# A two-layer hybrid decoder trunk on one core: DMAs of split-ahead weights issued by GpSimd instead of SyncE, and shorter steps in the first stage

## The chip, the cores and the metric

The kernel runs on one core of a Trainium2 chip. The metric is the device time of one execution in microseconds (us). Before the change the median of two runs is 2187.45 us (2185.61 to 2189.3). One more execution was profiled and took 2193.86 us; the profile's rows are of that one.

## The reference

Two decoder layers over 1024 tokens of width 1024, all in float32. Layer 0 mixes tokens by gated linear attention (GLA, 4 heads), layer 1 by sparse attention (an indexer chooses 256 keys per query, 16 heads). After each mixer comes a layer norm of the residual sum and a gated addition of a per-layer embedding `p`.

```python
# layer 0
h = x @ w_in                      # q, k: 1024 wide each; v, z: 2048 each; a: 16
g = log_sigmoid(a @ w_a2 + b_a) / 16
# per head, in chunks, state S (256 x 512):
o_c = q_c S + tril(q_c k_c^T) v_c ;  S = S * decay + k_c^T v_c
o = o * rsqrt(mean(o*o) + eps) * gn_g
y = (o * silu(z)) @ w_out
# layer 1
q, k, v, z, qi, ki, wi = split(x @ w_in)
score = sum_h relu(qi_h . ki) * wi_h ;  idx = top_k(score, 256)
y = (softmax(q . k[idx]) v[idx] * silu(z)) @ w_out
# after each
x = layer_norm(ALPHA * x + y)
x = x + (p[i] @ ple_w[i]) * sigmoid(x @ ple_gate_w[i])
```

## The kernel before, in words

**Precision.** TensorE multiplies in float32r. To keep float32's accuracy each operand is split into a high part (ScalarE copies it to float32r) and a low part (VectorE subtracts the high part), and each product is three matmuls: high by high, high by low, low by high. So every weight has to be loaded, split into two tiles and kept until it is used.

**Stages.** (1) The *front* (`front_phase`) multiplies x by the weights of q, k and most of z of layer 0 for all 1024 tokens. It does so in pairs of blocks (`class Pair`) by a Strassen-like scheme: seven products of 12 matmuls instead of eight, from sums and differences of operands. (2) *Layer 0* runs in two halves of 512 tokens (half 0, half 1), each over four heads. Head h has core steps (`core_steps`: scores `s1`, state `s2`, output `s3`, turning `s4`, for four chunks c of 128 tokens); between them run the v projection of head h+1 (`v_phase`) and the output projection of head h-1 (`out_phase`). Each half ends with the layer norm (`norm_steps`) and a tail; the tail of half 0 also holds small projections of layer 1. (3) *Layer 1* runs in two halves over 16 heads and two tails.

**Order of work.** Every engine executes its instructions in the order in which the program emits them, and SyncE (SP) issues all DMAs in such an order too: an instruction that waits holds up everything behind it on its engine or queue. The program emits TensorE's matmuls in sequence and keeps a clock of its own, `fl.now`, in units of estimated us: each matmul of 512 columns adds 512/2400 (line 60). All other work is placed by that clock: `after(dt, f)` emits f when the clock has moved on by dt; `req` puts a step off until its condition holds; pacers are called after each few matmuls.

- The *operand queue* of the front: for each pair 18 steps (allocation, sums, high parts, low parts, load), one emitted every `pacing["gap"]` units (line 1567: 1.3 from the third pair on). The queue is refilled with the steps of the next pair after product 1 of the running one (the third pair: after product 6). When a product needs an operand whose step has not yet been emitted, `todo` emits steps until it has.
- *Split-ahead* (`Weights.split_ahead`, lines 228 to 257) splits the 65 weight tiles of layer 1 and of its small projections, in order, in the background: 30 in the front (line 1581), one step every 1.4 units, and 35 in layer 0 (line 1670), every 2.06 units. For each half of a tile (a *cut*, 256 KB) it loads `pst` (three buffers), lets ScalarE write `phi` (line 248), stores `phi` to DRAM (line 250), loads the cut after the next (line 238), lets VectorE subtract (line 252) and stores the low part (line 254). Three steps per cut; `bg3.finish()` at the end of the front (line 1588) and of layer 0 (line 1761) emits whatever is left at once. Layer 1 then loads finished parts (line 176).
- *Kept parts* (line 205): the v and output weights of layer 0, split in half 0, are stored to DRAM for half 1: 32 tiles, two stores each.
- *Turning by DRAM* (`squares_out`, `squares_in`, `gate`; lines 724 to 752): for most chunks the output `ot` is stored to DRAM as `od` in four DMAs (line 727), read back turned as `uf` (line 733, two buffers) 4.0 units later, and gated by VectorE (line 752) another 4.0 units later. The other chunks are turned on TensorE in `s4` through the PSUM bank `oT`, which `v_phase` also uses.
- GpSimd computes `rs`, the scale of a head's output rows (lines 756 and 758, in `made`, when a turned block is ready; used at line 803), and `rstd` in the layer norms (lines 841 to 844), and clears some tiles (`wa2f` at line 1617, for instance).

At the start of layer 0 and for each head `g_load` (line 473) loads `wa2f`, from which the decays are made.

Of the kernel before, what the change touches and what calls it, by code (L numbers as in the profile page):

```python
# [144 lines left out]
class Weights:  # L145
# [16 lines left out]
    def step(self):  # L162
        n, i = self.ns, self.part
        if n == self.stop:
            return False
        whole = n not in self.staged and self.seq[n][0] in self.ahead
        if n >= self.nu + (3 if whole and self.seq[self.nu - 1][0][0] not in ("do", "o") else 2):
            return False
        if i == 0:
            if not whole:  # L170
                self.loads(n + 1)
            if n not in self.parts:
                self.reserve(n)
        if whole:
            for part, there in zip(self.parts[n], self.ahead[self.seq[n][0]]):
                self.nc.sync.dma_start(part.bitcast(F32), there)
            self.ns += 1
            self.loads(min(self.ns + 1, self.nu + 3))
            return True
        st = self.staged[n]  # L180
        hi, lo = self.parts[n]
        if n == 0:
            i = (0, 2, 1, 3)[i]
        c = slice((i % 2) * 512, (i % 2) * 512 + 512)
        key = self.seq[n][0]
        gain = None
        if key[0] == "o":
            row = 4 * key[1] + 2 * key[3] + i % 2
            gain = self.gains[:, row:row + 1]
        if i < 2:  # L190
            self.nc.scalar.activation(hi[:, c], st[:, c], AF.Copy, scale=1.0 if gain is None else gain)
        elif gain is None:
            self.nc.vector.tensor_sub(lo[:, c], st[:, c], hi[:, c].bitcast(F32))
        else:
            self.nc.vector.scalar_tensor_tensor(lo[:, c], st[:, c], gain, hi[:, c].bitcast(F32),
                                                op0=OP.mult, op1=OP.subtract)
        self.part = (self.part + 1) % 4
        if self.part == 0:
            if key in self.keep:
                there = [self.dram.tile([128, 1024], F32, name=x) for x in ("whs", "wls")]  # L200
                self.keep.remove(key)

                def store():
                    for x, part in zip(there, (hi, lo)):
                        self.nc.sync.dma_start(x, part.bitcast(F32))
                    self.ahead[key] = there
                self.after(1.6, store)
            self.staged.pop(n)
            self.ns += 1
            self.after(1.5, lambda: self.loads(self.ns + 2))  # L210
        return True
# [16 lines left out]
    def split_ahead(self, keys, pool, hi_pool):  # L228

        w = dict(self.seq)  # L230
        cuts = [(key, slice(c, c + 512)) for key in keys for c in (0, 512)]
        tiles = {}

        def load(i):
            if i < len(cuts):
                key, c = cuts[i]
                tiles[i] = pool.tile([128, 512], F32R, tag="pst", name="pst", bufs=3)
                self.nc.sync.dma_start(tiles[i].bitcast(F32), w[key][:, c])
        load(0)
        load(1)  # L240
        yield
        yield
        for i, (key, c) in enumerate(cuts):
            st = tiles.pop(i)
            if not c.start:
                there = [self.dram.tile([128, 1024], F32, name=n) for n in ("whs", "wls")]
            hi = hi_pool.tile([128, 512], F32R, tag="xst", name="phi", bufs=2)
            self.nc.scalar.activation(hi, st.bitcast(F32), AF.Copy)  # L248
            yield
            self.nc.sync.dma_start(there[0][:, c], hi.bitcast(F32))  # L250
            load(i + 2)
            self.nc.vector.tensor_sub(st, st.bitcast(F32), hi.bitcast(F32))  # L252
            yield
            self.nc.sync.dma_start(there[1][:, c], st.bitcast(F32))
            if c.start:
                self.ahead[key] = there
            yield

    def take(self, key):
# [33 lines left out]
def trunk_kernel(ctx, tc, x_tok, x_T, p_T, pos, freq, g_q, g_k, g_v, g_z, g_a, g_a2, g_ba, g_gn, g_o,  # L293
# [281 lines left out]
    def qk_phase(u):  # L575
# [23 lines left out]
            after(0.7, lambda: split(qh[:, 1], ql[:, 1], q[:, 1], done))  # L599
        chain((0, query(0)), (0.6, query(1)), (0.6, key(0)), (0.6, key(1)))  # L600

    def core_steps(u):
        h, half = u["h"], u["half"]
        v = u["v"]
# [84 lines left out]
        def s3(c):  # L689
            def f():  # L690
                cs = slice(c * 128, c * 128 + 128)
                fl.req(("A", c) in st, v[c] is not None, not has_state(c) or ("S", c) in st and "qhl" in u)
                fl.ripe(st["At", c] + 1.6)
                Ah, Al = st.pop(("A", c))
                vh, vl = v[c]
                ps = pp.tile([128, 512], F32, tag="o", name="o")
                ops = [(Ah, vh), (Al, vh), (Ah, vl)]
                if has_state(c):
                    qh, ql = u["qhl"]
                    for d, (sh, sl) in enumerate(st.pop(("S", c))):  # L700
                        ops += [(qh[:, d, cs], sh), (ql[:, d, cs], sh), (qh[:, d, cs], sl)]
                for i, (l, r) in enumerate(ops):
                    mm(ps, l, r, i == 0, i == len(ops) - 1)
                ot = lp.tile([128, 512], F32, tag="ot", name="ot", bufs=2)
                if by_square(c):
                    dve.transpose(ot.rearrange("p (m b i) -> p b m i", m=4, b=4), ps)  # L706
                    after(2.2, lambda: squares_out(c, ot))
                else:
                    dve.tensor_copy(ot, ps)
                junk = lp.tile([128, 512], BF16, tag="junk", name="junk")  # L710
                act.activation(junk, ps, AF.Square, accum_out=u["ss"][:, c:c + 1])  # L711
                st["o", c] = ot
                st["ot", c] = fl.now
                u["spent"].add(c)
                if c == 3:
                    u["late"] = True
                if c < 3:
                    after(0.3, lambda: make_S(c + 1))
            return f
# [4 lines left out]
        def squares_out(c, ot):  # L724
            od = dp.tile([4, 32, 4, 128], F32, tag="od", name="od", bufs=4)
            for a in range(4):
                nc.sync.dma_start(od[:, :, a].rearrange("m r x -> r m x"),
                                  ot[32 * a:32 * a + 32].rearrange("p (m x) -> p m x", m=4))

            def squares_in():  # L730
                fl.req(h == 0 or u["prev"].get("out", 0) > c)
                uf = lp.tile([128, 512], F32, tag="uf", name="uf", bufs=2)
                nc.sync.dma_start(uf, od.rearrange("m r a x -> (m r) (a x)"))
                after(4.0, lambda: gate(c, uf))
            after(4.0, squares_in)

        def gate(c, uf):
            fl.req("z" in u)
# [12 lines left out]
            z = u["z"][:, :, c * 128:c * 128 + 128].rearrange("p b (a i) -> p b a i", a=4)  # L751
            chain((0, lambda: dve.tensor_mul(turned, turned, z)), (0.8, high), (0.9, low))

        def made(c, uh, ul):
            rc = slice(c, c + 1)
            pool.tensor_scalar(u["rs"][:, rc], u["ss"][:, rc], ALPHA ** 2 / 512.0, ALPHA ** 2 * EPS,
                               op0=OP.mult, op1=OP.add)
            pool.tensor_tensor(u["rs"][:, rc], u["rs"][:, rc], mhalf[:, rc], op=OP.pow)
            u["u"][c] = uh, ul

        def s4(c):
            def f():
# [1 line left out]
                    return  # L764
                cs = slice(c * 128, c * 128 + 128)
                fl.req(h == GH - 1 or units[h + 1].get("turns"))
                fl.req(("o", c) in st, "z" in u, h == 0 or u["prev"].get("out", 0) > c)
                fl.ripe(st["ot", c] + 1.1)
                ot = st.pop(("o", c))
                ps = pp.tile([128, 4, 128], F32, tag="oT", name="oT")  # L770
                for b in range(4):
# [459 lines left out]
    def front_phase():  # L1231
# [332 lines left out]
        queue.extend([P[2].room, *P[2].steps(), *P[2].more_steps(), P[3].load])  # L1564
        fl.run(a.products(3))
        queue.extend(b.last_steps())
        pacing["gap"] = 1.3

        def last_load():
            W.stop = len(W.seq)  # L1570
# [1 line left out]
        for n in range(2, len(P)):  # L1572
            for name in (1, 2, 6, 7, 5, 4, 3):
# [4 lines left out]
                fl.run(P[n].products(name))  # L1578
                if name == (6 if n == 2 else 1):
                    if n == 2:  # L1580
                        bg3.set(W.split_ahead(later[:30], fp, xp), 1.4)
                    queue.extend(P[n].last_steps())
                    if n + 1 < len(P):
                        queue.extend([P[n + 1].room, *P[n + 1].steps(), *P[n + 1].more_steps()])
                    queue.append(P[n + 2].load if n + 2 < len(P) else last_load)
# [58 lines left out]
    for half in range(NH):  # L1644
# [15 lines left out]
        for h, u in enumerate(units):  # L1660
            if h == 0:
# [5 lines left out]
                    fl.run(z_last(14, hs), z_last(15, hs))  # L1667
                load_y()
                if half == 0:
                    bg3.set(W.split_ahead(later[30:], lp, xp), 2.06)  # L1670
            bulk, n = [], 0
            if h:
                bulk.append(out_phase(units[h - 1], y))
# [12 lines left out]
        ta = lp.tile([128, 2, HT], F32, tag="e1", name="pt")  # L1686
        Pt = load_p(0, half, lambda: t2k("ah", F32R, 4), 7.0, lambda k: ta[:, k])
        norm, y_done = norm_steps(y, lp, EPS / ALPHA ** 2)
        fl.run(out_phase(units[-1], y, norm))
        if half:  # L1690
            bg.finish()
# [545 lines left out]
```

## Time and profile before

| | before |
|---|---|
| median of 2 runs | 2187.45 us |
| profiled execution, its own time | 2193.86 us |
| span of the profile | 2192.1 us |
| TensorE busy | 1953.6 us (89%) |
| VectorE busy | 1558.7 us (71%) |
| ScalarE busy | 968.3 us (44%) |
| GpSimd busy | 51.2 us (2%) |
| mean granted TensorE clock | 0.955 |
| bytes moved by DMA | 550.44 MB, all issued by SyncE |

How to read the rows: in a table of stretches each stands with its length, then busy time and number of instructions of each engine, the granted TensorE clock, the share of the 16 DMA engines that was busy, and GB/s. A timeline row is start, duration, engine, line, operation, output<-input, and in brackets how long the engine was idle before it and what ended that. A row of waits is "who waited <- for whom: us in total, times, longest". A group's row has busy time and mean ns of one, then idle time before it. PE is TensorE, PEld its weight loads, DVE VectorE, ACT ScalarE, POOL GpSimd, SPq the DMA queue of SyncE. L59 is the line of every matmul.

### The profile page before, as it was taken

How to read it: one execution, taken by the hardware profiler on the slowest of the kernel's cores; microseconds unless marked ns; L12 is line 12 of the kernel's file. 1: busy time of each engine (PE TensorE's matmuls, PEld its weight loads, DVE VectorE, ACT ScalarE, POOL GpSimd, SP SyncE). 2: the span in 40 equal slices, each digit the busy share in tenths (PEclk: the TensorE clock that was granted, in tenths of full speed). 3: DMA queues.
4: the chain of work that ended last, by engine and by line, in shares of the span. 5: the costliest groups of instructions: out<-in, count | busy, mean ns of one | idle time of the engine just before them, and what ended most of it. 6: DMA issues, size and time to landing. Idle time of an engine off the chain costs nothing.

```text
span 2192.1 us, 26677 instructions
## 1 busy us (share of the span) xinstructions
PE 1953.6 (89%) x8764; PEld 1594.4 (73%) x8764; DVE 1558.7 (71%) x3138; ACT 968.3 (44%) x1852; POOL 51.2 (2%) x114
## 2 busy tenths in 40 slices
PE   7888988597697999877875999999999999999999
PEld 5676766475485788756764888888887888888877
DVE  5675656367567868676679589877778788777773
ACT  4232334254444545443332455866654254434332
POOL 0000000000000100000000000000000000000000
PEclk8899999898898999998988999999999999999999
DMA  5276676787797787867752476877887699888983
GB/s 194 92 256 235 235 239 236 248 318 247 257 319 256 285 296 264 291 203 252 264 189 78 150 244 209 299 280 260 298 277 252 228 358 329 290 284 289 302 306 135
DMA packets 222156, 550.44 MB, mean 251 GB/s; under 512 B 25281, under 2 KB 38593, under 8 KB 215873
## 3 DMA queue, kind: packets, MB, share of 16 engines
q1 hardware_dynamic: 222016, 548.73, 72.5%
q8 instruction: 69, 1.13, 0.2%
q14 instruction: 71, 0.57, 0.1%
HBM read 359.76 MB, written 190.97 MB: 251 GB/s over the span
## 4 chain that ended last, share of the span: by engine, by line
PE 66%; DMA 13%; DVE 13%; ACT 4%; issue 3%; SPq 2%; DVEq 0%; ACTq 0%
PE pb L59 51%; PE o L59 5%; PE S L59 5%; DMA wls<-pst 3%; DMA uf<-od 2%; PE U L59 1%; DMA wa2f<-in_g_a 1%; DMA whs<-phi 1%; DVE tkj L1114 1%; DVE pst L252 1%; DMA pst<-in_d_q 1%; DMA xst<-x2s 1%; DVE v L420 1%; DVE wlo L1389 1%; DVE y L803 1%
## 5 line engine op out<-in xcount | busy, mean ns | idle before, releaser
L59 PE MATMUL pb<-x,whi 128*128 128x512 f32 x1552 | 489.0, 396 | 11.0 <-DVE v L420 6.4
L59 PE MATMUL pb<-whi,u 128*128 128x512 f32 x1024 | 353.5, 406 | 35.0 <-DVE v L420 33.0
L59 PEld LDWEIGHTS pb<-x,whi 128*128 128x128 f32 x1552 | 287.7, 190 | 66.3 <-DVE v L420 6.8
L59 PE MATMUL pb<-x,wlo 128*128 128x512 f32 x776 | 307.1, 396 | 20.2 <-DVE wlo L1389 20.2
L59 PEld LDWEIGHTS pb<-whi,u 128*128 128x128 f32 x1024 | 199.8, 195 | 79.3 <-DVE v L420 35.1
L59 PE MATMUL pb<-wlo,u 128*128 128x512 f32 x512 | 205.8, 402 | 1.5 <-DMA wlo<-wls 1.5
L59 PEld LDWEIGHTS pb<-x,wlo 128*128 128x128 f32 x776 | 147.6, 190 | 57.0 <-DVE wlo L1389 24.9
L1897 ACT ACTIVATE sq<-P,mx 128x128 f32<-128x128 f32 (+7 forms) x128 | 98.9, 773 | 88.8 <-DVE mx L1890 63.4
L59 PE MATMUL pb<-whi,x 128*128 128x512 f32 x384 | 131.1, 396 | 3.6 <-DVE y L803 3.4
L59 PE MATMUL S<-kT,q 128*128 128x512 f32 (+2 forms) x576 | 122.5, 342 | 0.0
L252 DVE TENSOR_TENSOR pst<-pst,phi 128x512 fp32r<-128x512 f32 x130 | 88.8, 683 | 39.9 <-ACT phi L248 39.9
L711 ACT ACTIVATE junk<-o 128x512 bf16<-128x512 f32 x32 | 19.1, 597 | 219.9 <-DVE ot L706 125.6
L1943 ACT ACTIVATE ph<-PT 128x512 fp32r<-128x512 f32 (+2 forms) x160 | 86.5, 558 | 66.0 <-PE o L59 44.5
L59 PEld LDWEIGHTS pb<-wlo,u 128*128 128x128 f32 x512 | 100.3, 196 | 20.4 <-DMA wlo<-wls 1.9
L59 PEld LDWEIGHTS S<-kT,q 128*128 128x128 f32 x576 | 100.9, 188 | 18.1 <-DVE mx L1890 0.7
L1941 DVE TENSOR_TENSOR PT<-PT,ph 128x512 fp32r<-128x512 f32 (+2 forms) x160 | 93.4, 594 | 22.1 <-ACT ph L1943 21.7
L248 ACT ACTIVATE phi<-pst 128x512 fp32r<-128x512 f32 x130 | 80.6, 623 | 50.7 <-DMA pst<-in_d_z 25.7
L1158 ACT ACTIVATE tk<-sc,tki 128x768 f16<-128x768 f32 (+2 forms) x90 | 92.7, 1031 | 18.1 <-DVE tki L1167 15.8
L1903 DVE STREAM_TRANSPOSE sq<-sq 128x128 f32<-128x128 f32 (+7 forms) x128 | 97.6, 768 | 3.2 <-ACT sq L1897 3.1
L59 PE MATMUL o<-ph,vT 128*128 128x512 f32 (+2 forms) x320 | 92.5, 370 | 0.0
L59 PEld LDWEIGHTS pb<-whi,x 128*128 128x128 f32 x384 | 73.0, 190 | 20.0 <-DVE y L803 4.3
L1890 DVE CUSTOM_DVE_ANT_0 P<-S,bias 128x512 f32<-128x512 f32 (+3 forms) x128 | 71.0, 560 | 12.5 <-PE S L59 10.0
(412 smaller groups left out, 4043.4 us busy)
## 6 DMA issues: line engine op xcount, KB each, us to landing
whi<-whs SPq DMA_DIRECT2D x160, 512.0 KB
wlo<-wls SPq DMA_DIRECT2D x160, 512.0 KB
sqd<-sq SPq DMA_DIRECT2D x192, 256.0 KB
PT<-sqd SPq DMA_DIRECT2D x48, 1024.0 KB
whs<-phi SPq DMA_DIRECT2D x130, 256.0 KB
wls<-pst SPq DMA_DIRECT2D x130, 256.0 KB
whs<-whi SPq DMA_DIRECT2D x32, 512.0 KB
wls<-wlo SPq DMA_DIRECT2D x32, 512.0 KB
```

Of the source, the lines that this page charges most:

```text
L59: self.pe.matmul(out, lhsT, rhs, start=start, stop=stop)
L248: self.nc.scalar.activation(hi, st.bitcast(F32), AF.Copy)
L252: self.nc.vector.tensor_sub(st, st.bitcast(F32), hi.bitcast(F32))
L420: dve.tensor_sub(lo, src, hi.bitcast(F32))
L803: dve.scalar_tensor_tensor(ys, ps, rs[:, t:t + 1], ys, op0=OP.mult, op1=OP.add)
L1114: dve.tensor_scalar(junk()[:, :n], scs[j], thr_ap, None, op0=op, op1=OP.add, accum_out=cnt[:, j:j + 1])
L1158: act.activation(junk()[:, :n], scs[j], AF.Sign, bias=cand[:, j:j + 1].bitcast(F32), accum_out=cnt[:, j:j + 1])
L1890: dve.tensor_tensor_reduce(P[:, a:a + e], ps[:, :e], bias_t[T][:, a:a + e], op0=OP.add, op1=OP.min, scale=-ATTN_SCALE, scalar=lim, accum_o ...
L1897: act.activation(to, rows, AF.Exp, scale=-1.0, bias=mx, accum_out=sm[:, t:t + 1])
L1903: dve.transpose(x, x)
L1941: dve.tensor_sub(lo, lo.bitcast(F32), hi.bitcast(F32))
L1943: chain((0, lambda: act.activation(hi, lo.bitcast(F32), AF.Copy)), (0.8, second))
```

## The change

Nothing of the computation changes. It

- issues all DMAs of split-ahead (load, store of the high part, store of the low part) and the stores of kept parts from GpSimd's queue instead of SyncE's; a kept part is stored 2.0 units after its split instead of 1.6;
- in split-ahead puts the load of cut i+2 behind the store of the low part of cut i, where it stood behind the store of the high part;
- sets the gap of the front's operand queue to 0.95 (was 1.3) and splits 26 keys in the front and 39 in layer 0 (were 30 and 35);
- makes `rs` 1.5 units after the output `o` of the chunk (`scale`) instead of when the turned block is ready;
- counts turned blocks under way (`turning`): `squares_in` and `s4` start only when fewer than two are; reads `uf` back 3.5 units after its store (was 4.0) and gates it 5.5 units later (was 4.0);
- holds split-ahead back from the last output phase of each half for 4 * B + 4.0 = 24.5 units (B is 5.12).

```diff
@@ Weights.step
                 def store():
                     for x, part in zip(there, (hi, lo)):
-                        self.nc.sync.dma_start(x, part.bitcast(F32))
+                        self.nc.gpsimd.dma_start(x, part.bitcast(F32))
                     self.ahead[key] = there
-                self.after(1.6, store)
+                self.after(2.0, store)
@@ Weights.split_ahead
-                self.nc.sync.dma_start(tiles[i].bitcast(F32), w[key][:, c])
+                self.nc.gpsimd.dma_start(tiles[i].bitcast(F32), w[key][:, c])
...
-            self.nc.sync.dma_start(there[0][:, c], hi.bitcast(F32))
-            load(i + 2)
+            self.nc.gpsimd.dma_start(there[0][:, c], hi.bitcast(F32))
             self.nc.vector.tensor_sub(st, st.bitcast(F32), hi.bitcast(F32))
             yield
-            self.nc.sync.dma_start(there[1][:, c], st.bitcast(F32))
+            self.nc.gpsimd.dma_start(there[1][:, c], st.bitcast(F32))
             if c.start:
                 self.ahead[key] = there
+            load(i + 2)
             yield
@@ core_steps
+    turning = [0]
...
                 st["ot", c] = fl.now
+                after(1.5, lambda: scale(c))
...
             def squares_in():
-                fl.req(h == 0 or u["prev"].get("out", 0) > c)
+                fl.req(h == 0 or u["prev"].get("out", 0) > c, turning[0] < 2)
+                turning[0] += 1
...
-                after(4.0, lambda: gate(c, uf))
-            after(4.0, squares_in)
+                after(5.5, lambda: gate(c, uf))
+            after(3.5, squares_in)
...
-        def made(c, uh, ul):
+        def scale(c):
             rc = slice(c, c + 1)
             pool.tensor_scalar(u["rs"][:, rc], u["ss"][:, rc], ALPHA ** 2 / 512.0, ALPHA ** 2 * EPS,
                                op0=OP.mult, op1=OP.add)
             pool.tensor_tensor(u["rs"][:, rc], u["rs"][:, rc], mhalf[:, rc], op=OP.pow)
+
+        def made(c, uh, ul):
+            turning[0] -= 1
             u["u"][c] = uh, ul
@@ s4
-                fl.req(("o", c) in st, "z" in u, h == 0 or u["prev"].get("out", 0) > c)
+                fl.req(("o", c) in st, "z" in u, h == 0 or u["prev"].get("out", 0) > c, turning[0] < 2)
                 fl.ripe(st["ot", c] + 1.1)
+                turning[0] += 1
@@ front_phase
-        pacing["gap"] = 1.3
+        pacing["gap"] = 0.95
...
-                        bg3.set(W.split_ahead(later[:30], fp, xp), 1.4)
+                        bg3.set(W.split_ahead(later[:26], fp, xp), 1.4)
@@ layer 0
-                    bg3.set(W.split_ahead(later[30:], lp, xp), 2.06)
+                    bg3.set(W.split_ahead(later[26:], lp, xp), 2.06)
...
         norm, y_done = norm_steps(y, lp, EPS / ALPHA ** 2)
+        bg3.due = max(bg3.due, fl.now + 4 * B + 4.0)
         fl.run(out_phase(units[-1], y, norm))
```

## The prediction

> **What bounds the kernel now.** I read the page's first lines, then busy time by stretch; I cut the span where the stages change.
>
> ```profile
> span 2192.1 us, 26677 instructions
> PE 1953.6 (89%) x8764; PEld 1594.4 (73%) x8764; DVE 1558.7 (71%) x3138; ACT 968.3 (44%) x1852; POOL 51.2 (2%) x114
> ```
> ```profile
> core 0: us, PE busy (x) PEld busy (x) DVE busy (x) ACT busy (x) POOL busy (x), PEclk, DMA share, GB/s
> 144.00:404.00 260.00, 222.47 (x938) 175.16 (x939) 154.76 (x236) 90.88 (x155) 0.75 (x4) 0.99 0.70 237
> 404.00:440.00 36.00, 13.16 (x51) 10.13 (x50) 9.19 (x17) 9.25 (x15) 0.00 (x0) 0.70 0.75 261
> 440.00:760.00 320.00, 260.61 (x1125) 210.36 (x1124) 224.19 (x413) 150.30 (x289) 18.83 (x40) 0.90 0.82 283
> 880.00:1160.00 280.00, 230.30 (x997) 187.00 (x998) 196.53 (x459) 104.97 (x209) 12.75 (x32) 0.91 0.71 242
> 1360.00:2192.00 832.00, 820.81 (x3902) 683.51 (x3900) 626.82 (x1372) 401.75 (x816) 11.39 (x21) 1.00 0.80 279
> ```
>
> TensorE (PE) bounds the kernel and is idle for 2192.1 - 1953.6 = 238.5 us. The last 832 us hold only 11 of them: layer 1 has nothing to give. The front stage from 144 us on holds 37.5, its end 22.8, the two stretches of layer 0 where the heads run 59.4 + 49.7 = 109.1. The change touches these, so 169 us is all that it can win by removing idle time.
>
> Next, how each stretch loses its time. In the front, the chain that ended last, over one pair:
>
> ```profile
> 180.39 10.74 PE pb L59 x46
> 191.76 1.23 DVE wlo L1389
> 193.04 5.34 PE pb L59 x22
> 199.00 0.69 DVE wlo L1405
> 199.74 2.58 PE pb L59 x10
> 203.55 0.70 DVE s3l L1405
> 204.29 10.74 PE pb L59 x46
> ```
> ```profile
> 763.81 50.53 PE pb L59 x222
> ```
> ```profile
> PE pb L59 <- DVE wlo L1389: 20.2, 11, 3.8
> PE pb L59 <- DVE s3l L1405: 18.3, 12, 2.1
> ```
>
> A pair takes 204.29 - 180.39 = 23.9 us. Three times PE waits for a low part that VectorE (DVE) has only just made: that of block 1 (line 1389), of product 6 and of product 7 (line 1405). Unhindered, a matmul takes 50.53 / 222 = 0.228 us, so the 84 of a pair 19.1: 4.8 us per pair is lost.
>
> At the end of the front, the timelines of PE, ACT and SyncE's queue (SP):
>
> ```profile
> 436.70 1.22 PE L59 MATMUL U<-ah,w 96*128 96x512 f32 x2 [22.73 <-DVE w L420]
> ```
> ```profile
> 421.84 0.63 ACT L248 ACTIVATE phi<-pst 128x512 fp32r<-128x512 f32 x1 [8.68 <-DMA pst<-in_d_q]
> ```
> ```profile
> 418.73 0.33 SPq L238 DMA_DIRECT2D pst<-in_d_q  x1
> 432.75 1.31 SPq L473 DMA_DIRECT2D wa2f<-in_g_a  x3
> ```
>
> PE has started on layer 0 and then stands for 22.73 us until `w` is made from `wa2f`. That load stands in SP's queue behind the rest of the keys that `bg3.finish()` pushes out (line 1588), whose loads wait for their buffers.
>
> In layer 0, SP's own waits, then one junction between heads, on SP, DVE and PE:
>
> ```profile
> SPq L238 <- DMA wls<-pst: 172.1, 70, 6.8
> SPq L250 <- ACT phi L248: 119.9, 37, 11.3
> SPq L254 <- DVE pst L252: 67.3, 43, 4.6
> ```
> ```profile
> 579.47 0.35 SPq L238 DMA_DIRECT2D pst<-in_d_o  x1
> 580.46 0.32 SPq L733 DMA_DIRECT2D uf<-od  x1
> ```
> ```profile
> 586.20 0.69 DVE L752 TENSOR_TENSOR uf<-uf,z 128x512 f32<-128x512 f32 x1 [9.86 <-DMA uf<-od]
> ```
> ```profile
> 590.04 0.80 PE L59 MATMUL pb<-whi,u 128*128 128x512 f32 x1 [12.87 <-DVE v L420]
> 601.08 1.12 PE L63 MATMUL oT<-ident,ot 128*128 128x128 f32 x4 [8.11 <-DVE v L420]
> ```
> ```profile
> DVE uf L752 <- DMA uf<-od: 59.1, 15, 9.9
> PE pb L59 <- DVE v L420: 39.4, 6, 12.9
> PE oT L63 <- DVE v L420: 45.5, 6, 8.7
> ```
>
> SP waits 172.1 + 119.9 + 67.3 = 359 us in all at the three DMAs of split-ahead, in order, with everything else queued behind. Here the turned block `uf` is fetched only after the key's load got its buffer (579.47). DVE stands 9.86 us at `uf`, everything behind it on DVE is late, among it the evacuation `v`, and PE stands for a bank: 12.87 us, then 8.11 once more. The first kind sums to 39.4 us, the second to 45.5.
>
> **The change part by part.**
>
> Shorter steps in the front (gap 1.3 to 0.95, line 1567). The kernel's clock adds 512/2400 = 0.2133 per matmul (line 60), so a pair is 84 x 0.2133 = 17.9 units long. A pair has 18 queued steps: 1 room, 9, 5 more, 2 last, 1 load. At 1.3 they want 23.4 units, more than there is; the backlog stays, and `todo` pushes each operand out just before its product. At 0.95 they want 17.1: no backlog. Counted from the refill of the queue, block 1's low part is the 8th step, at 7.6, and needed after six products, at 15.4; product 7's is the 17th, at 16.2, needed at 23.0. Each comes about 7 units early, against waits of about 2 us. DVE has room: 154.76 us of work in 222. I let 4.5 of the 37.5 us stay and count **33 saved**; at least 15, if the waits move to another operand, at most the 37.5.
>
> Fewer keys in the front (30 to 26). A cut (half a key) is three steps of 1.4 units, so 60 cuts want 182 steps and 52 want 158. From product 6 of the third pair on, the front has 4 products, 12 pairs and 32 matmuls of `gates`, 10 + 215 + 7 = 232 units, or 166 steps. So now some six cuts are left for the finish, and then none. Together with the move of these DMAs off SP this frees `wa2f`, though the memset of `wa2f` (line 1617) then stands on GpSimd's queue behind the last stores. **18 of the 22.73 us saved**; at least 10, since a landing of `wa2f` behind other loads can be slow, as this row of the chain has it:
>
> ```profile
> 459.00 9.46 DMA wa2f<-in_g_a
> ```
>
> Moved DMAs. 130 cuts have a load and two stores each, 390 DMAs, and 32 kept parts two stores, 64: 454 go from SP to GpSimd. On SP that frees the 359 us of waits and 454 issues of 0.33 us, but what comes of it is bounded by the junction: `od` cannot be issued before SP has passed its other loads and `uf` not before `od` has landed. In the junction above only the step from 579.47 on is sure. The gate is also sent 1.0 unit later (3.5 + 5.5 against 4.0 + 4.0), so that DVE does other work meanwhile. I take two thirds of the 59.1 us of waits as removed, 40, and three in four of these on PE's path: **30 saved**. Lower bound 0 (see the second rival). Upper bound 85, both kinds of PE's waits gone. I do not count the second kind, because it also comes without a late `uf`:
>
> ```profile
> 929.37 0.68 DVE L752 TENSOR_TENSOR uf<-uf,z 128x512 f32<-128x512 f32 x1
> 944.59 1.11 PE L63 MATMUL oT<-ident,ot 128*128 128x128 f32 x4 [7.41 <-DVE v L420]
> ```
>
> Fewer stalls also lift the granted clock, 0.90 and 0.91 in these stretches against 0.99 in the front; matmuls straight after a stall took 0.80 us. I put **4 us** on it, between 0 and 15.
>
> What GpSimd pays. No DMA was issued there before. Below is SP's 0.32 us per issue (the `uf` row), above GpSimd's longest operation, its nearest row of an instruction that writes much:
>
> ```profile
> L2106 POOL MEMSET sq<- 128x2048 f32 (+1 forms) x2 | 5.3, 2668 | 131.6 <-PE pb L59 74.2 <-DVE bias L1187 57.4
> L758 POOL TENSOR_TENSOR rs<-rs,mhalf 128x1 f32<-128x1 f32 x32 | 18.5, 578 | 2.7
> ```
>
> I take 1.0 us, nearer to the small instruction. A cut in the front comes every 4.2 units, 4.2 x 19.1 / 17.9 = 4.5 us, and would hold GpSimd for 3: it fits. The load of cut i+2 now stands after the second store of cut i and waits for the store of i-1, sent a whole cut before, so ScalarE (ACT) sees it four steps later, 6 us: small waits, inside the 7 units of lead. Cost 0; without that cover see the fourth rival. Queued behind these waits on GpSimd are only `rs` and `rstd`; `rs` is now made 1.5 units after the scores, long before line 803 needs it, and split-ahead pauses 24.5 units at the last output phase, where `rstd` is on the path. That `squares_in` and `s4` wait for fewer than two turned blocks keeps SP from standing at a full `uf`; 0.
>
> Eight cuts more in layer 0: 8 x 0.68 us on DVE, half of it in junctions, **-3**. The last cut now stands here:
>
> ```profile
> L248 ACT ACTIVATE phi<-pst x38: 612/620/643, 762.0 to 1128.0; 128x512 fp32r<-128x512 f32 x38
> ```
>
> Eight cuts at 6.2 units and the pause, or two of them, put it 74 to 98 units later, to the end of half 1's tail, where up to three cuts may be pushed out by the finish before layer 1: **-2**, at worst -12.
>
> Sum: 33 + 18 + 30 + 4 - 3 - 2 = 80. The profiled execution took 2193.86 us, so 2114; the runs' median is 6.4 us lower, so **2107 us**.
>
> The Trainium skill speaks against the third term: by "DMA: Bandwidth & Descriptors", section "Issuing engines are not separate DMA queues", DMAs of all engines run on the same 16 engines, and issuing from another saves only the time to initiate them. The row of 172.1 us says that on SP waits in order, not initiation, is what costs. By the rule the sum would be 46, by the rows 80.
>
> **The rivals.**
>
> 1. The move to GpSimd wins nothing: the round trip of `od` and `uf` and the shared transfer engines set the time, not SP's order. For it: `uf` took 5.7 us after its issue (586.20 - 580.46) and the share of DMA is 0.82. Against it: 70 waits at line 238. Sum 33 + 18 - 3 - 2 = 46: 2141. The rule of the Trainium skill above comes to the same.
>
> 2. The lag of DVE was SP's doing altogether, and both kinds of PE's waits go: 33 + 18 + 85 + 15 - 5 = 146: 2041. Against it: the row at 944.59.
>
> 3. The steps of the front are no faster in effect: PE still waits, since ACT and DVE stand in order at late `pst` loads (8.68 us above). Then 18 + 30 + 4 - 5 = 47: 2140.
>
> 4. Slower: GpSimd issues too slowly. From 4.5 / 3 = 1.5 us per issue it falls behind in the front; then ACT waits for `pst` in order, and all operands with it. At the upper row, 2.67 us, a cut takes 8.0, and 52 take 416 us. They start where they start now:
>
> ```profile
> L248 ACT ACTIVATE phi<-pst x60: 612/624/636, 110.4 to 429.9; 128x512 fp32r<-128x512 f32 x60
> ```
>
> From 110 us they last until 526, where the forecast has the front done by 437 - 33 - 18 = 386: 140 us later, 2107 + 140 = 2247. It begins to cost at 276 / 156 = 1.8 us per issue (386 - 110 us for 52 x 3 issues) and is slower than before from (276 + 80) / 156 = 2.3. For it: three of four rows of GpSimd are tiny, none is a DMA. Against it: only the longest row passes 1.5.
>
> The Trainium skill's "SBUF — State Buffer", section "Who interferes with whom", bears on it: descriptors of GpSimd's DMAs need a port that some operations of VectorE lock. No run here shows it yet.
>
> **How the numbers follow.** Forecast 0.55, first rival 0.17, second 0.12, third 0.06, fourth 0.10. The likeliest gives 2107. Two per cent, about what a measurement of this kernel can tell from no change, is 44 us: below 2144 is faster. The forecast with its bounds gives 0.53 faster, the first rival and the third 0.13 of their 0.23, the second all: 0.78. Slower is the fourth, 0.10 less a little of it near its threshold: 0.09. The rest, 0.13, lies within. The range reaches from the second rival to 2155, past the first and the third: 2040 to 2155; it leaves out the fourth and the edges.
>
> **What would show it.** Right: in the front, pairs of 19 to 20 us without the three waits at 1389 and 1405; no stand of 20 us before `U<-ah,w`; SP's waits at 238, 250 and 254 gone and found on GpSimd's queue; DVE's 59.1 us at `uf` down to about 20; PE's second wait at `oT` still there; a GpSimd issue near 1 us. Wrong: `phi` waiting for `pst` by the hundred us; PE's idle time in 440 to 1160 unchanged; PE's idle time at the start of layer 1 above 10 us; DVE's mean times longer than the 680 to 690 ns of such rows now.

## The result, and the profile after

The median after the change is 2089.44 us (2087.2 to 2091.68, two runs), 98 us less than before: 0.9552 of it, with a 95% interval of 0.9496 to 0.9608. Both profiled executions, 2193.86 and 2087.2 us, give 107 us; the places below are measured in them.

First the head of the page of the changed kernel, then its busy time by stretch, and for comparison three stretches of the kernel before. The cuts lie at the same work: layer 0's first matmul `U<-ah,w`, the same matmul at the start of half 1, and the 21 us wait of the transposes `xt`, which open the tail of half 1. The last stretch so holds that tail (53 us before, 54 after) and layer 1.

```profile
span 2085.1 us, 26854 instructions
...
PE 1940.2 (93%) x8764; PEld 1592.4 (76%) x8764; DVE 1553.6 (75%) x3138; ACT 968.8 (46%) x1852; POOL 304.2 (15%) x568
```
```profile
144.00:340.00 196.00, 192.81 (x845) 157.72 (x844) 135.71 (x212) 80.19 (x135) 68.19 (x126) 1.00 0.82 282
340.00:376.00 36.00, 27.20 (x109) 21.33 (x107) 16.62 (x29) 11.97 (x22) 8.85 (x19) 0.91 0.85 287
376.00:765.00 389.00, 353.38 (x1577) 290.52 (x1578) 294.06 (x529) 203.24 (x380) 112.98 (x209) 0.95 0.83 295
765.00:1092.00 327.00, 267.52 (x1155) 216.20 (x1153) 251.33 (x606) 128.10 (x245) 72.26 (x136) 0.91 0.66 231
1092.00:2085.00 993.00, 981.08 (x4632) 815.11 (x4632) 756.66 (x1621) 493.16 (x991) 27.85 (x49) 1.00 0.79 272
```
```profile
437.00:858.00 421.00, 361.61 (x1577) 293.85 (x1577) 295.37 (x531) 205.03 (x383) 18.83 (x40) 0.92 0.81 281
858.00:1199.00 341.00, 266.26 (x1155) 216.16 (x1155) 251.58 (x605) 125.86 (x242) 16.77 (x40) 0.90 0.64 216
1199.00:2192.00 993.00, 980.00 (x4632) 814.94 (x4632) 750.92 (x1611) 488.11 (x982) 13.21 (x22) 1.00 0.77 265
```

PE does the same matmuls and is idle for 2085.1 - 1940.2 = 144.9 us, where it was 238.5. Everything up to layer 0's first matmul takes 60 us less, layer 0 up to its last tail takes 32 + 14 = 46 us less, and the rest takes 993 us both times. In the front (144 to 340) PE is now idle for 3.2 us of 196; 845 matmuls there make 0.232 us for one, so 84, a pair, take 19.5 us instead of 23.9.

The waits of PE and DVE that the prediction went by, and those of GpSimd's queue:

```profile
POOL whs L250 <- ACT phi L248: 240.3, 80, 48.4
POOL wls L253 <- DVE pst L251: 223.3, 78, 26.0
POOL pst L238 <- DMA wls<-pst: 63.1, 29, 6.0
PE oT L63 <- DVE v L420: 45.7, 6, 9.5
DVE uf L756 <- DMA uf<-od: 15.2, 7, 4.5
PE pb L59 <- DVE v L420: 7.2, 2, 6.1
PE pb L59 <- DVE wlo L1397: 4.2, 3, 2.1
PE pb L59 <- DVE s3l L1413: 2.6, 2, 1.5
```

The waits for low parts (20.2 and 18.3 us before) are down to 4.2 and 2.6, DVE's at `uf` from 59.1 to 15.2, and PE's first kind of wait, for `v`, from 39.4 to 7.2. GpSimd now stands where SP stood: 240.3 + 223.3 + 63.1 us. PE's second kind of wait, at `oT`, is as long as it was (45.5).

At the end of the front, PE's timeline:

```profile
376.34 0.72 PE L59 MATMUL U<-ah,w 96*128 96x512 f32 x2 [2.55 <-DVE w L420]
```

The 22.73 us stand there is 2.55. Last, the groups of split-ahead: ACT's high part and GpSimd's two stores.

```profile
L248 ACT ACTIVATE phi<-pst 128x512 fp32r<-128x512 f32 x130 | 81.3, 625 | 117.0 <-DMA pst<-in_d_z 26.4 <-DMA pst<-in_d_q 24.5 <-DMA pst<-in_d_o 23.9
L250 POOL DMA_DIRECT2D whs<-phi x130 | 72.6, 559 | 277.9 <-ACT phi L248 240.3 <-ACT Ah L662 32.2 <-ACT kh L656 3.2
L253 POOL DMA_DIRECT2D wls<-pst x130 | 71.5, 550 | 260.1 <-DVE pst L251 223.3 <-DVE kl L420 15.7 <-DVE Af L654 6.7
```

An issue holds GpSimd for 0.55 to 0.56 us. ACT's idle time ahead of `phi` is 117.0 us; it was 50.7.

### The profile page after: what moved, and what is told of

Read it like the earlier page. It is cut to its first block, busy times and chain, and to the rows that moved or that the text cites. A ratio compares the mean times of both kernels' runs of the same rounds, so it can differ in the third digit from the quotient of the medians.

```text
span 2085.1 us, 26854 instructions
## 1 busy us (share of the span) xinstructions
PE 1940.2 (93%) x8764; PEld 1592.4 (76%) x8764; DVE 1553.6 (75%) x3138; ACT 968.8 (46%) x1852; POOL 304.2 (15%) x568
## 4 chain that ended last, share of the span: by engine, by line
PE 55%; DVE 10%; DMA 7%; issue 6%; ACT 3%; POOL 1%; SPq 1%; DVEq 0%; ACTq 0%; POOLq 0%
PE pb L59 39%; PE o L59 6%; PE S L59 6%; DMA uf<-od 2%; PE U L59 1%; DMA wa2f<-in_g_a 1%; DMA wlo<-wls 1%; DVE tkj L1122 1%; DMA od<-ot 1%; DVE m L511 1%; DMA wls<-pst 1%; DVE y L811 1%; DVE v L420 1%; DVE bn L855 1%; DVE pst L251 0%
## 5 line engine op out<-in xcount | busy, mean ns | idle before, releaser
L248 ACT ACTIVATE phi<-pst 128x512 fp32r<-128x512 f32 x130 | 81.3, 625 | 117.0 <-DMA pst<-in_d_z 26.4
L849 POOL TENSOR_SCALAR rstd<-mv 128x1 f32<-128x1 f32 x16 | 5.8, 365 | 842.2 <-DVE mv L858 839.4
L250 POOL DMA_DIRECT2D whs<-phi x130 | 72.6, 559 | 277.9 <-ACT phi L248 240.3
L253 POOL DMA_DIRECT2D wls<-pst x130 | 71.5, 550 | 260.1 <-DVE pst L251 223.3
```

What stands on the lines that cost most here:

```text
L250: self.nc.gpsimd.dma_start(there[0][:, c], hi.bitcast(F32))
L253: self.nc.gpsimd.dma_start(there[1][:, c], st.bitcast(F32))
```

## The experiments

Every run was timed beside the kernel before on the same chip (2188.46, 2190.99 and 2188.44 us there). In the table the front ends at the first `U<-ah,w`, and layer 0 lasts from there to the end of the 21 us wait at `xt`, with which the tail of half 1 begins; both come from each run's profile. The changed kernel profiled twice gave 376.3 and 379.3 for the front, 715.9 and 716.5 for layer 0: differences under 4 us say little. The profile of the kernel before is of an execution 6.4 us above its median, so gains against that profile look some us larger than they do by the medians.

| kernel | median us | ratio [95%] | front ends | layer 0 |
|---|---|---|---|---|
| before | 2187.45 | 1 | 436.7 | 762.5 |
| after | 2089.44 | 0.9552 [0.9496, 0.9608] | 376.3 | 715.9 |
| after, again | 2089.73 | 0.9543 [0.9520, 0.9567] | 379.3 | 716.5 |
| after, old gap | 2129.89 | 0.9737 [0.9711, 0.9763] | 419.3 | 721.3 |
| after, DMAs on SP | 2091.18 | 0.9552 [0.9529, 0.9575] | 368.7 | 722.6 |
| after, 30 keys | 2110.68 | 0.9645 [0.9620, 0.9670] | 398.9 | 714.1 |
| after, old gate | 2102.41 | 0.9611 [0.9585, 0.9637] | 378.1 | 727.3 |
| after, on SP, old load place | 2111.99 | 0.9643 [0.9612, 0.9674] | 397.4 | 717.4 |
| after, four chunks by DRAM | 2110.91 | 0.9632 [0.9606, 0.9658] | 379.7 | 739.7 |
| after, slow issues | 2297.95 | 1.0488 [1.0463, 1.0512] | 477.4 | 813.7 |
| before, move alone | 2160.91 | 0.9867 [0.9841, 0.9894] | 440.3 | 724.6 |
| before, gate alone | 2172.55 | 0.9923 [0.9901, 0.9945] | 437.5 | 737.5 |
| before, gap alone | 2170.28 | 0.9915 [0.9893, 0.9937] | 418.3 | 756.6 |
| after, front on SP, layer 0 on GpSimd | 2084.51 | 0.9517 [0.9493, 0.9540] | 372.8 | 717.0 |

**The gap undone.** From the kernel after:

```diff
-        pacing["gap"] = 0.95
+        pacing["gap"] = 1.3
```

> The changed kernel with the gap of the front's operand queue back at 1.3; all else as changed. Theory (the gap alone ends the front's waits): the three waits per pair at lines 1397 and 1413 are back, the first U<-ah,w comes about 40 us later than the 376 us of the changed kernel, and the time is about 2129 us. Rival (the front gained because SyncE's queue was freed and operands were no longer held up by it): the waits stay away, the first U<-ah,w within 10 us of 376, the time within 10 us of 2089.

It lost 40 us by the medians; in its profile the front is 43 us longer, and PE's three waits there are back:

```profile
PE pb L59 <- DVE wlo L1397: 20.2, 11, 3.8
PE pb L59 <- DVE s3l L1413: 18.6, 12, 2.1
...
PE pb L59 <- DVE wlo L1413: 7.4, 6, 1.5
```

The gap is the cause of these waits, as the prediction had it; that it acts by a backlog of operand steps is the prediction's count of the steps.

**The DMAs back on SP.** From the kernel after, lines 205, 238, 250 and 253; the load stays behind the store of the low part:

```diff
-            self.nc.gpsimd.dma_start(there[0][:, c], hi.bitcast(F32))
+            self.nc.sync.dma_start(there[0][:, c], hi.bitcast(F32))
```

> The changed kernel with all DMAs of split-ahead and of kept parts issued by SyncE again (the load still behind the low part's store); all else as changed. Theory (SyncE's waits in order made uf late): SyncE again waits some 300 us at lines 238, 250 and 253, VectorE some 45 to 60 us at uf, PE's waits of the first kind are back, the time is 2120 to 2135 us. Rival (the later gate and the smaller number of blocks under way did it, the issuing engine nothing): the time is within 8 us of 2089 although SyncE's waits are back.

No loss: 0.9552 against 0.9552 and 0.9543. The theory, by which the move carried layer 0, falls. SP waits again at the three DMAs:

```profile
SPq L253 <- DVE pst L251: 93.4, 65, 5.8
SPq L250 <- ACT phi L248: 89.7, 48, 6.0
...
SPq L238 <- DMA wls<-pst: 37.5, 21, 4.3
```
```profile
DVE uf L756 <- DMA uf<-od: 5.8, 6, 3.0
```

But 220.6 us in place of 359, hardly at the load, and DVE waits only 5.8 us at `uf`. The front is 8 to 11 us shorter than with GpSimd, layer 0 some 6 longer: what the move still does for layer 0, the front takes back.

**The keys put back.** From the kernel after, `later[:26]` and `later[26:]` to 30:

```diff
-                        bg3.set(W.split_ahead(later[:26], fp, xp), 1.4)
+                        bg3.set(W.split_ahead(later[:30], fp, xp), 1.4)
```

> The changed kernel with 30 keys in the front and 35 in layer 0, as before. Theory (the stand at the end of the front was the load of wa2f behind the finish, and now the clearing of wa2f stands behind the finish on GpSimd): eight more cuts are pushed out at the end, PE waits 10 to 22 us before the first U<-ah,w instead of 2.6, the time is 2097 to 2110 us. Rival (with the finish off SyncE's queue the number of keys does not matter): PE waits under 6 us there and the time is within 6 us of 2089.

It lost 21 us, all in the front. PE's timeline there, and the row of GpSimd that `w` hangs on:

```profile
376.66 0.79 PE L59 MATMUL pb<-whi,x 128*128 128x512 f32 x1 [10.11 <-DVE pc L1489]
398.89 1.22 PE L59 MATMUL U<-ah,w 96*128 96x512 f32 x2 [12.61 <-DVE w L420]
```
```profile
392.38 0.33 POOL L1625 MEMSET wa2f<- 128x256 f32 x1
```

With the DMAs on GpSimd the rest of the keys still holds up `w`, now by way of the memset of `wa2f`, which comes on GpSimd's queue right after the last store of split-ahead (391.56) and right before the load of `wa2f` (392.74). That is half of the loss. The other half is the stand of 10.11 us (1.40 in the changed kernel): the cuts that the finish pushes out also stand in order on DVE, which waits twice for their `phi`, 3.06 and 3.70 us, ahead of the front's last evacuations `pc`.

**The old gate.** From the kernel after, read back and gated after 4.0 units each, and no limit on turned blocks:

```diff
-                after(5.5, lambda: gate(c, uf))
-            after(3.5, squares_in)
+                after(4.0, lambda: gate(c, uf))
+            after(4.0, squares_in)
```

> The changed kernel with uf read back 4.0 units after its store and gated 4.0 units later, as before, and without the limit of two turned blocks under way; rs is still made early and all DMAs are on GpSimd as changed. Theory (the move off SyncE carries most of layer 0's gain, the timing a smaller part): VectorE waits 25 to 35 us at uf instead of 15, the time is 2093 to 2105 us. Rival (the timing did it): VectorE waits about 59 us at uf as before the change, the first kind of PE's waits is back, the time is 2120 us or more.

13 us lost, as the theory had it; DVE's wait at `uf` rose to more than it said:

```profile
DVE uf L756 <- DMA uf<-od: 40.0, 12, 5.9
```

Which of the three does it, the earlier read, the later gate or the limit, this run does not tell.

**SP with the old load place.** From the kernel with the DMAs on SP, the load of cut i+2 goes back behind the store of the high part:

```diff
             self.nc.sync.dma_start(there[0][:, c], hi.bitcast(F32))
+            load(i + 2)
...
                 self.ahead[key] = there
-            load(i + 2)
```

> All DMAs on SyncE as in the run with SyncE, and besides the load of cut i+2 back behind the store of the high part, as before the change; gap, keys and gate as changed. The run with SyncE took 2091 us and SyncE waited only 37.5 us at line 238. Theory (it is the place of the load that freed SyncE, not the other engine): SyncE's wait at the load is back at 120 us or more, VectorE waits over 25 us at uf, layer 0 loses and the time is 2102 to 2120 us. Rival (the place of the load is worth nothing, the later gate covers it): within 7 us of 2091.

20 us lost, as the theory had it, but in another place: the front is 28.8 us longer and layer 0 is 5.2 shorter. SP's largest wait in this run is at the load, and DVE waits at `uf` as the theory said:

```profile
SPq L238 <- DMA wls<-pst: 219.0, 89, 7.2
```
```profile
DVE uf L756 <- DMA uf<-od: 25.9, 12, 3.9
```

Yet layer 0 is no longer for it: 717.4 us with 25.9 us at `uf`, 722.6 with 5.8. In this run a wait of that size at `uf` does not reach the time.

What stands behind that load on SP in the front are the loads of the pairs' own weights, `wst`. Waits from 110 to 360 us in this kernel:

```profile
DVE t L1369 <- DMA wst<-in_g_z: 39.7, 7, 7.2
ACT whi L1390 <- DMA wst<-in_g_z: 34.7, 6, 7.1
...
PE pb L59 <- DVE wlo L1397: 14.5, 9, 3.0
```

In the kernel with the DMAs on SP and the new load place, the same stretch:

```profile
DVE t L1369 <- DMA wst<-in_g_z: 22.9, 6, 4.7
ACT whi L1390 <- DMA wst<-in_g_z: 19.6, 6, 4.0
```

**The move alone.** From the kernel before, the same four lines to `nc.gpsimd`, the load in its old place:

```diff
-            self.nc.sync.dma_start(there[0][:, c], hi.bitcast(F32))
+            self.nc.gpsimd.dma_start(there[0][:, c], hi.bitcast(F32))
```

> The kernel before with only the issuing engine changed: split-ahead and kept parts on GpSimd, everything else as before (gap 1.3, 30 keys, gate after 4.0 + 4.0, load behind the high part's store). Theory (the move and the new place of the load take the same waits from SyncE, so either one does it alone): VectorE waits 30 to 45 us at uf instead of 59, layer 0 gains 20 to 30 us, the front nothing, its end up to 10: 2150 to 2168 us. Rival (the move is worth nothing in any company): within 9 us of 2188.

30 us gained, with layer 0 37.9 us shorter in the profile and the front 3.6 longer. Of its waits:

```profile
POOL pst L238 <- DMA wls<-pst: 292.6, 95, 8.6
```
```profile
DVE uf L752 <- DMA uf<-od: 28.8, 11, 6.9
```
```profile
440.31 1.22 PE L59 MATMUL U<-ah,w 96*128 96x512 f32 x2 [24.99 <-DVE w L420]
```

The stand at the load has gone to GpSimd, where `uf` isn't behind it. The stand at the boundary has only changed queues: 24.99 us.

**The gate alone.** From the kernel before, the reading back, the gate and the limit as in the change:

```diff
-                after(4.0, lambda: gate(c, uf))
-            after(4.0, squares_in)
+                after(5.5, lambda: gate(c, uf))
+            after(3.5, squares_in)
```

> The kernel before with only the turning changed: uf read back after 3.5 units, gated 5.5 units later, fewer than two turned blocks under way; all DMAs on SyncE, rs made late, gap and keys as before. Theory, new (VectorE's stand at uf can be taken away from either end, by an earlier uf or by a later gate; the run with only the move gained 30 us, mostly in layer 0): VectorE waits under 35 us at uf instead of 59, layer 0 gains 20 to 40 us, the front nothing: 2148 to 2168 us. Rival (with all DMAs on SyncE the later gate needs the early rs or the pause beside it): within 8 us of 2189.

16 us gained, less than the theory said, more than the rival. The waits at layer 0:

```profile
PE oT L63 <- DVE v L420: 66.6, 6, 14.8
DVE uf L755 <- DMA uf<-od: 42.0, 12, 6.6
PE pb L59 <- DVE v L420: 9.4, 3, 6.2
```

PE's first kind of wait fell from 39.4 to 9.4 us, but the second rose from 45.5 to 66.6 and took back 21 of these 30.

**The gap alone.** From the kernel before, 1.3 to 0.95:

> The kernel before with only the gap of the front's operand queue at 0.95. Theory, new (on SyncE with the load behind the high part's store, each load stands in front of the weights' loads; the run with that place of the load lost 29 us of the front): the three low parts no longer stop TensorE, but about half of the 40 us is lost to later weights: the first U<-ah,w at 412 to 425 us, the time 2163 to 2175 us. Rival (the gap brings its 40 us alone): first U<-ah,w near 397, the time 2145 to 2155 us.

18 us gained, as the theory had it, of the 40 that the gap is worth beside the rest of the change. Of the three waits for low parts those at line 1405 are all but gone, that at line 1389 stays (18.2 us from 105 us to the boundary before, 15.1 here). Its waits from 110 to 400 us are almost those of the kernel on SP with the old load place:

```profile
DVE t L1361 <- DMA wst<-in_g_z: 39.4, 7, 7.8
ACT whi L1382 <- DMA wst<-in_g_z: 34.3, 6, 7.8
...
PE pb L59 <- DVE wlo L1389: 15.1, 9, 2.7
```

Shorter steps can't make an operand of weights that SP has not yet loaded. Besides, the end of the front takes part of the gain back, for it still has 30 keys and now comes sooner: PE waits 7.0 us for `s4h`, then for an evacuation that stands on DVE behind split-ahead, and 14.54 us for `w`:

```profile
393.72 0.80 PE L59 MATMUL pb<-whi,x 128*128 128x512 f32 x1 [8.95 <-DVE pc L1481]
```

**Without the bank `oT` between heads.** From the kernel after, all four chunks of heads 0 to 2 are turned by DRAM:

```diff
-            return c < (3 if h < GH - 1 else 2 + half)
+            return c < (4 if h < GH - 1 else 2 + half)
```

> The changed kernel with the fourth chunk of heads 0 to 2 turned by DRAM too (by_square for c under 4 instead of 3), so that these heads use no TensorE transposes and no oT bank for turning. Theory (the waits of the second kind, 46 us in six places, are TensorE in order standing at a bank that the v projection has not given back): the waits at oT fall to under 10 us, some of them come back as waits for the bank elsewhere, the time is 2050 to 2075 us. Rival (VectorE's lag at the junction is what costs, whoever waits for it): TensorE waits as long at the next instruction that needs VectorE, the time is within 8 us of 2089.

Some 20 us slower (0.9632 against 0.9552 and 0.9543), which neither the theory nor the rival had. PE's waits in layer 0:

```profile
PE pb L59 <- ACT u L750: 28.2, 8, 7.1
PE tr L59 <- DVE m L585: 26.7, 9, 7.5
...
PE oT L63 <- DVE ot L711: 1.6, 1, 1.6
```

The waits at `oT` are gone, and longer ones stand elsewhere, for `u` (1.2 us in the changed kernel) and `m` (3.6). Either the bank is only where the lag of DVE and ACT shows, or the fourth chunk's way through DRAM costs as much as the bank did; the run does not tell these apart.

**Slow issues.** From the kernel after, three powers of one column on GpSimd ahead of each of the 454 DMAs, whose results nothing uses:

```diff
+    def issue(self, out, src):
+        for i in range(3):
+            self.nc.gpsimd.tensor_tensor(self.pad[:, i + 1:i + 2], self.pad[:, 0:1], self.mhalf[:, 0:1], op=OP.pow)
+        self.nc.gpsimd.dma_start(out, src)
```

> The changed kernel with three small GpSimd operations (128x1 power, 0.58 us each by the profile before) ahead of each of its 454 DMAs, so that one issue holds GpSimd for about 0.55 + 1.7 = 2.3 us instead of 0.55. By the prediction's working, 2.3 us per issue makes the front's 52 cuts last 156 x 2.3 = 359 us from 105 us on, to 464, where U<-ah,w came at 376: the time would be about 2089 + 88 = 2177 us, with ScalarE waiting for pst. Rival (GpSimd has slack and the pacing takes it up): under 20 us, 2109 us at most.

```profile
L160 POOL TENSOR_TENSOR pad<-pad,mhalf 128x1 f32<-128x1 f32 x476 | 278.0, 604 | 3.4
```
```profile
105.00:477.00 372.00, 289.61 (x1117) 222.78 (x1115) 187.07 (x287) 107.41 (x180) 364.49 (x638) 0.91 0.54 195
```

Both rows are of the stretch from 105 to 477 us: 476 / 3 = 159 issues in 364 us of work, 2.3 us for one, as intended (the records overlap a little, so their means add up to more). The kernel is slower than before by 4.9%. In the front GpSimd is busy for 364 of 372 us and sets its length: 105 + 156 x 2.3 = 464 by the working of the fourth rival, 477 measured. That working stopped there; layer 0 lost another 98 us, and the time is some 120 us above the 2177 expected. By which waits layer 0 falls behind is not followed here.

**The front on SP, layer 0 on GpSimd.** From the kernel after, `split_ahead` gets its queue from the caller:

```diff
-                        bg3.set(W.split_ahead(later[:26], fp, xp), 1.4)
+                        bg3.set(W.split_ahead(later[:26], fp, xp, nc.sync), 1.4)
...
-                    bg3.set(W.split_ahead(later[26:], lp, xp), 2.06)
+                    bg3.set(W.split_ahead(later[26:], lp, xp, nc.gpsimd), 2.06)
```

> The changed kernel with split-ahead issued by SyncE in the front and by GpSimd in layer 0, kept parts on GpSimd. Theory (the front is faster on SyncE, where loads and stores land sooner, layer 0 on GpSimd): the first U<-ah,w near 369 us instead of 376, layer 0 as in the changed kernel, the time 2080 to 2085 us. Rival (the two queues only trade the same waits): within 3 us of the changed kernel run beside it.

> The changed kernel once more, on the same chip as the three others of this call: 2086 to 2093 us by its first measurement; every theory expects the same.

The fastest median, 5.2 us below the changed kernel timed beside it, with a layer 0 like that of the changed kernel and a front between those of the two queues, not at the 369 of the theory. The intervals of the ratios overlap, so that it is faster is not settled.

## Why the prediction was right, and where it was wrong

The time, 2089, lies in the range and 18 us under the forecast of 2107. In the profile the front and the boundary gave 60 us (forecast 33 + 18 = 51) and layer 0 gave 46 (forecast 30 + 4 - 3 - 2 = 29). The sum came nearly right, with luck: layer 0's gain was booked on the move, and parts that the sum held at nothing bring it without the move as well.

1. *Shorter steps, 33.* Mechanism right: undone, the waits for low parts come back. The size is 40 beside the rest and 18 by itself. The working did not see that the step depends on others: the front must not keep 30 keys, and SP must not stand at split-ahead's load while the pairs' weights are behind it. On SP the new load place does that (20 us), and off SP the question doesn't arise.

2. *Fewer keys, 18.* Right in size: 21. The prediction named the memset of `wa2f` behind the last stores as what remains; the stands of 12.61 and 24.99 us show it. It did not name the second stand, 10.11 us with 30 keys, where the finish's cuts hold up the front's last evacuations on DVE.

3. *The move, 30.* **This is the step that failed**: "On SP that frees the 359 us of waits ... 30 saved". The wait that it meant to remove did go: PE's first kind fell by 32.2 us. But the move is not what removed it. Alone the move gives 30 us, so the mechanism is there: with `uf` off the queue that stands at the load, DVE's waits fall from 59.1 to 28.8 us. But beside the rest it gives nothing in the time, some 6 us in layer 0 against 4 to 11 in the front. The gate 5.5 units after an earlier read, with the limit, which the prediction counted only as an aid to this term, is a second cure of the same stand: 16 us alone, 13 beside the rest. With the rest and on SP, layer 0 takes 722.6 us, with the old load place even 717.4, so neither the move nor the load place is needed there. Nor does a shorter wait at `uf` always pay: below some 26 us it moves layer 0 no further (25.9 us in the run with 717.4, 15.2 in the changed kernel with 715.9, 5.8 in the run with 722.6). Of the 762.5 - 717.4 = 45 us gained in that run's layer 0, the gate alone accounts for 25 by its own profile (16 by the medians). The keys add nothing to it (714.1 with 30 in the front). How the rest divides between the early `rs`, the pause before the last output phase and what the parts do together stays open; no run has one of these two alone.

4. *The second kind of waits, 0.* Right: 45.5 and 45.7 us. The run with all chunks by DRAM shows that this cure at the bank moves the wait and does not end it.

5. *Clock, 4.* Too small: PE's busy time for the same 8764 matmuls fell by 1953.6 - 1940.2 = 13.4 us. In layer 0, for which the 4 was meant, it fell by 8.2 in half 0 (granted clock 0.92 and 0.95) and rose by 1.3 in half 1; the front, for which nothing was counted, gave 7.5 (0.99 and 1.00 in its main stretch). That all of this is the clock's doing is not shown.

6. *Eight cuts more, -3, and the end of split-ahead, -2.* Both 0. DVE's busy time in layer 0 did not grow (295.37 + 251.58 before, 294.06 + 251.33 after); ten of its instructions more stand in the last stretch (1621, 1611 before), whose length is the same. The added cuts stand not between the heads but in the tail of half 1: nine `phi` from 1096 us on, the last just after layer 1's first matmul, which did not wait:

```profile
1148.91 0.61 ACT L248 ACTIVATE phi<-pst 128x512 fp32r<-128x512 f32 x1
```
```profile
1146.09 0.61 PE L59 MATMUL pb<-x,whi 128*128 128x512 f32 x2
```

7. *What GpSimd pays, 1.0 us per issue and 0 in the front.* An issue took 0.55, and the cost was not 0: the front ends at 376.3 and 379.3 us, with its DMAs on SP at 368.7 and 372.8, so it is 4 to 11. ACT's idle time ahead of line 248, most of it for `pst`, which the prediction called small, is 117.0 us (50.7 before), with 99.7 on SP. `phi` waiting by the hundred us was named as a sign of being wrong; it came, and did not cost what the fourth rival said. That this wait is all of the difference between the queues is not shown.

The rivals. The first was half right. The move wins nothing in company, which is what the Trainium skill's rule ("DMA: Bandwidth & Descriptors", "Issuing engines are not separate DMA queues") says; but its reason, that the round trip of `od` and `uf` sets the time and not SP's order, holds at most in part: with the gate where it was, the move alone took DVE's wait at `uf` from 59.1 to 28.8 us. The 30 us of the move alone are more than that rule leaves, for what was saved is a wait in order. The second rival failed on the waits at `oT`, the third on the front's 3.2 us of idle time. The fourth was right in kind and too mild: at 2.3 us per issue, where its working makes the changed kernel as fast as the one before, it is slower by 4.9%, because layer 0 falls behind too. Its lower points, 1.5 and 1.8 us, were not run.

## What to carry to other kernels

Before DMAs are moved to another queue, name the transfer that is late behind them, and ask whether a later consumer, or the waiting DMA put further back, cures the same lateness: here two cures of one stand did not add up. So measure each part both alone and out of the whole; here 30 and 0 (the move) mark substitutes, 18 and 40 (the gap) parts that need each other. A queue of steps that is emitted by a clock must want less time than the work that it feeds.

## What the runs showed of the hardware

- The DMAs issued by GpSimd held it for 0.54 to 0.56 us each, loads and stores of 256 KB and stores of 512 KB alike, beside a DVE that was 75% busy; DVE's subtraction for `pst` took 683 ns before and after. The Trainium skill ("SBUF — State Buffer", "Who interferes with whom") has some DVE operations lock the port that such descriptors need; no stall of that kind shows in this kernel's rows, but whether its DVE operations are of the locking kind was not tested.
- A GpSimd operation on 128x1 elements cost about as much as one DMA issue there: three of them in a row took 1.59 to 1.67 us, 0.53 to 0.56 each, beside 0.58 to 0.59 for the issue behind them (from 201 to 207 us of the run with slow issues; the single records, 627 ns on average, overlap).
- The time from issue to landing of GpSimd's 256 KB stores had a median of about 5 us, by the list of DMA issues after:

```profile
whs<-phi POOLq DMA_DIRECT2D x130, 256.0 KB, 4.9
wls<-pst POOLq DMA_DIRECT2D x130, 256.0 KB, 5.1
```
